# Sparse-attention and pooling block: one wide query projection, a padded value tile, probabilities scaled on GpSimd, weight-sum copies on the SyncE queue

## The chip, the core and the metric

The kernel runs on one core of one Trainium2 chip. The metric is device time in microseconds (us) of one execution; lower is better. TensorE (PE in the profile) multiplies matrices, VectorE (DVE), ScalarE (ACT) and GpSimd (POOL) work element by element, and DMAs are issued here by SyncE (SP) and by GpSimd, each in the order of its queue.

## What is computed

One decoder layer on x of 1024 positions by 1024 channels, all in float32. Attention has 8 query heads over 2 key/value heads and three branches; a pooling mixer runs beside it; both are gated, projected, added to x, and a squared-ReLU MLP of width 4096 follows.

```
h = rms_norm(x); proj = h @ w_in          # queries, 6 key/value sets, gates, pooling input, merge gates
a = g0*softmax(q k_cmp) v_cmp + g1*softmax(q k_sel) v_sel + g2*softmax(q k_win) v_win
a = a @ w_branch_attn
b = pool_mixer(u_pool) @ w_branch_pool    # trailing means over 2/4/8/16, group maps
x = x + (sigmoid(ga)*a + sigmoid(gb)*b) @ w_out
x = x + square(relu(rms_norm(x) @ w_ff1)) @ w_ff2
out = rms_norm(x)
```

With 16 blocks of 64 positions and 16 selected blocks, the selected branch is plain causal attention here, and the kernel computes it so.

## The kernel before

**Precision.** Each float32 operand is split in a high part (cast to fp32r by ACT) and a low part (the rest, by a subtraction), and `mm3` (lines 77 to 79) does three matmuls for one product: high by high, high by low, low by high. The helper `load` (L163 to L183) fetches a weight tile of 128x512 into a ring `wraw` of 4 buffers (L178), casts it to `whi` (L179) and subtracts to `wlo` (L82, on VectorE or, by default, on GpSimd); `whi` and `wlo` have 3 buffers each.

**Stages, in the order of time.** (1) Keys and values of four branches for all positions, and the row norms. (2) `block2` and `compress`: the other keys and values, and the two compressing MLPs. (3) `qblock(0)` and `qblock(1)`: the queries, 256 columns each; for every tile t of 128 positions 24 matmuls with a 256-column moving weight, then ACT scales the result into `q` (L394), GpSimd rotates it (`rope`, L145 to L149), and SP stores it in DRAM (`qd`). `keys` (rotation on VectorE, a transpose L362, a split) is called in the first pass only. (4) The pooling mixer and its gate `gb`, m = 0 to 7. (5) Attention: 32 pairs (i, hp), i being the block of 128 queries and hp the pair of heads. Query tiles come back from DRAM (`load_q`, L543) and are transposed and split by `split_q`. For each pair, `units_a` makes scores (L557, L558, masks L560), the row maxima (L567, VectorE), the exponentials (L568, ACT), and then scales the probabilities by gate over sum: selected ones in L624 and compressed ones in L625 on VectorE, window ones in L626 on ACT. `units_b` of the same pair then transposes the probabilities in blocks of 128 (L652), splits them (L655 ACT, L656 VectorE), and multiplies by the values (L663). The last block takes the compressed values `vch`, a tile of 64 rows (a "64x256" matmul on 64 of the array's rows). Pair n's `units_b` is interleaved with pair n+1's `units_a`. As filler, the merge gate `ga` is projected beside it: 128 terms of three 512-column matmuls each (`ga_terms`, tile `psG`), handed out by `advance` in proportion to the work done. (6) Branch projection, merge (`ta` and `gb` come back from DRAM, L803 and L804) and `w_out`, whose residual is loaded straight into `acc` (L817). (7) The MLP, in a scheme with 7 instead of 8 block products that needs sums of weight blocks.

**Weight sums.** `weight_sums` makes these sums by DMA alone, 32 tiles of 1 MB: a 16-byte token (L209, SP), which makes the step wait for a place in the program, then a DRAM to DRAM copy (L210, GpSimd queue), and one step later an accumulating DMA (L215, GpSimd queue). Seven steps run beside the pooling gate, 25 beside attention.

**What sets the order.** The program is written as above; the tile framework's scheduler then sets the order of each engine's instructions, and every engine runs its own list in that order. Pools give and take back on-chip memory; a tile waits until the one that lay there before has been read.

Of the kernel before, what the change touches and what calls it, by code (L numbers as in the profile page):

```python
# [49 lines left out]
def build(tc, a, out, dbg=None):  # L50
# [87 lines left out]

    def rope(eng, v, nh, cos, sin, wk):
        cb = cos[:, None, None, :].to_broadcast([P, nh, 2, 8])  # L140
        sb = sin[:, None, :].to_broadcast([P, nh, 8])
        A = wk.tile([P, 8, 2, 8], F32, name="ropeA", bufs=2)[:, :nh]
        B = wk.tile([P, 8, 2, 8], F32, name="ropeB", bufs=2)[:, :nh]
# [20 lines left out]
    def load(src, lo_eng=None, blk=None):  # L164
        _, na, n = src.shape
        step = min(na, HALF // n) if blk is None else 1
        his, los = [], []
        for a0 in range(0, na, step):
            w = step * n
            raw = strm.tile([P, HALF], F32, tag="wraw", name="wraw", bufs=RAWS)  # L170
            if blk is None:
                hi = strm.tile([P, HALF], F32R, tag="whi", name="whi", bufs=HILO)
                lo = strm.tile([P, HALF], F32R, tag="wlo", name="wlo", bufs=HILO)
            else:
                hi = blk.tile([P, 280], F32R, tag="bhi", name="bhi", bufs=10)
                lo = blk.tile([P, 280], F32R, tag="blo", name="blo", bufs=10)
# [10 lines left out]
    vst = [vk.tile([P, NT, NG, P], F32R, name=f"vst{b}") for b in range(2)]  # L187
    vch = vk.tile([DH, NG, P], F32R, name="vch")
    kds = vk.tile([P, NG, NCB + S], F32R, name="kds")
# [91 lines left out]
    with ExitStack() as st:  # L281
        psF = pool(st, "psF", bufs=4, space=PSUM)
        psH = pool(st, "psH", bufs=2, space=PSUM)
        wkA = pool(st, "wkA", side="right")

        def compress(kv):
            X = wkA.tile([P, 16, NG, NCB], F32, name="X")
            Xh = wkA.tile([P, 16, NG, NCB], F32R, name="Xh")
            Xl = wkA.tile([P, 16, NG, NCB], F32R, name="Xl")
            nc.gpsimd.memset(X[DH:P, :, :, NCB - 1:NCB], 0.0)  # L290
# [57 lines left out]
            else:  # L348
# [6 lines left out]
                for g in range(NG):  # L355
                    nc.vector.tensor_copy(vch[:, g], f(vh[g * DH:(g + 1) * DH]))

# [27 lines left out]

        def qblock(b):
            w = block_w(b * 256, 256)
            for t in range(NT):
                sl = slice(t * P, (t + 1) * P)
                ps = psF.tile([P, HALF], F32, name="psF")  # L390
                mm3(ps[:, :256], [(XH[k][:, sl], XL[k][:, sl], w[0][:, k], w[1][:, k])
                                  for k in range(NK)])
                q = wkA.tile([P, 4, 2, DH], F32, name="q", bufs=2)
                nc.scalar.activation(q, dup(ps[:, :256].rearrange("p (h d) -> p h d", d=DH)), AF.Copy,  # L394
                                     scale=req[:, t:t + 1])
                rope(nc.gpsimd, q.rearrange("p h e d -> p (h e) d"), 8, cosT[:, t], sinT[:, t], wkA)
                nc.sync.dma_start(qd[t][:, b * 512:(b + 1) * 512], q.rearrange("p h e d -> p (h e d)"))
# [13 lines left out]
        nc.vector.tensor_scalar(sg, sg, 0.5, 0.5, op0=MUL, op1=ADD)  # L411
        qblock(0)
        qblock(1)
        dump("kds", f(kds))
# [5 lines left out]
    kvctx.close()  # L420
    blkctx.close()


    with ExitStack() as st:
# [6 lines left out]
        with ExitStack() as st2:  # L431
# [79 lines left out]
    with ExitStack() as st:  # L511
# [13 lines left out]
        def ga_terms():  # L525
            for m in range(NK):
                gh, gl = load(cols(a["w_in"], C_GA + m * P, P))
                for hf in range(2):
# [10 lines left out]
                    yield  # L539

        def load_q(i, g):
            qi = wk.tile([P, HALF], F32, name="qi", bufs=2)
            nc.sync.dma_start(qi, qd[i][:, g * HALF:(g + 1) * HALF])  # L543
            return qi

# [47 lines left out]
        def unit_win(u, e):  # L593
# [19 lines left out]
            if e == 1:  # L613
# [22 lines left out]
        def units_b(u):  # L636
            i, hp, g, nw, w0 = (u[n] for n in ("i", "hp", "g", "nw", "w0"))
            blocks = [(u["pS"], NCB + b * P, vst[0][:, b, g], P) for b in range(i + 1)]
            blocks += [(u["pW"], b * P, vst[1][:, w0 + b, g], P) for b in range(nw // P)]
            blocks.append((u["pS"], 0, vch[:, g], NCB))  # L640
            o = oacc[:, hp % 2]
# [4 lines left out]
            def tr(gi):  # L646
                bl = groups[gi]
                n = len(bl)
                ps = psT.tile([P, HALF], F32, name="psT").rearrange("p (b e n) -> p b e n", b=2, e=2)
                for j, (src, c0, _, _) in enumerate(bl):  # L650
                    for e in range(2):
# [7 lines left out]
            def pv(gi):  # L659
                ph, pl = parts.pop(gi)  # L660
                for part in (ph, pl):
                    for j, (_, _, v, rows) in enumerate(groups[gi]):
                        nc.tensor.matmul(o, lhsT=v, rhs=part[:rows, j], start=gi == 0 and j == 0 and part is ph,  # L663
                                         stop=2 * gi + j == nb - 1 and part is pl)
# [22 lines left out]
        done, given, summed = 0.0, 0, 0  # L687

        def advance(w):
            nonlocal done, given  # L690
# [353 lines left out]
```

## Time and profile before

| what | us |
|---|---|
| median of 3 runs (lowest, highest) | 1493.94 (1491.46, 1497.39) |
| the profiled execution's own time | 1493.06 |
| its span | 1491.3 |
| PE, DVE, ACT, POOL busy | 1443.1, 1006.1, 759.2, 154.1 |

The span is the time from the first to the last recorded instruction. The profiled execution's own time is 1.8 us longer than its span, and stands 0.9 us below the median. Matmuls are pipelined: the recorded length of one is longer than the distance to the next, so distances between starts are read as its price.

### The profile page before, as it was taken

To read this page: it belongs to the slowest core of one execution; us is meant where nothing else is said; L and a number is where in the kernel's file an instruction comes from. 1 tells how busy PE (TensorE), PEld (TensorE's weight loads), DVE (VectorE), ACT (ScalarE), POOL (GpSimd) and SP (SyncE) were. 2 spreads that over 40 slices of the span, in tenths; PEclk is the share of its full clock that TensorE was granted. 3 is DMA by queue.
4 is the path that set the end of the run, shared out by engine and by line. 5 is a ranking of instruction groups with operands and counts; after the bars stand their busy time and mean duration, and the time that the engine had idled before them with its cause. 6 is when DMAs were issued, how large, how long until landed. Compare 5 with 4: busy or idle time off the path is not lost.

```text
span 1491.3 us, 20797 instructions
## 1 busy us (share of the span) xinstructions
PE 1443.1 (97%) x7385; PEld 1193.7 (80%) x7385; DVE 1006.1 (67%) x1950; ACT 759.2 (51%) x1559; POOL 154.1 (10%) x214
## 2 busy tenths in 40 slices
PE   8899999998999999999899999999999999999996
PEld 6788888886778887787688888888888888888885
DVE  5793461115888888787657658667897376669995
ACT  4454231124778877776334454575344454764451
POOL 2006423331111111111000000000000000000000
PEclk9999999999999999999999999999999999999998
DMA  8234217875768678766955332333233233333323
GB/s 309 69 100 149 71 43 189 215 202 132 201 156 212 153 187 196 171 169 150 327 174 162 108 97 91 100 100 99 85 106 97 94 99 93 99 94 97 98 80 113
DMA packets 130233, 204.67 MB, mean 137 GB/s; under 512 B 9936, under 2 KB 62928, under 8 KB 129616
## 3 DMA queue, kind: packets, MB, share of 16 engines
q1 hardware_dynamic: 112064, 136.22, 29.7%
q0 software_dynamic: 17920, 67.11, 19.9%
q8 instruction: 58, 0.95, 0.2%
q14 instruction: 47, 0.39, 0.1%
q10 hardware_dynamic: 144, 0.00, 0.0%
HBM read 186.52 MB, written 83.89 MB: 181 GB/s over the span
## 4 chain that ended last, share of the span: by engine, by line
PE 87%; DVE 5%; DMA 3%; ACT 2%; issue 1%; POOL 0%; SPq 0%; DVEq 0%; ACTq 0%; POOLq 0%
PE psm L79 16%; PE psm L77 16%; PE psm L78 16%; PE oacc L663 6%; PE psF L78 5%; PE psF L79 5%; PE psF L77 5%; PE psT L652 4%; PE psS L557 3%; PE psS L558 2%; PE psG L77 2%; PE psG L78 2%; PE psG L79 2%; DMA gb<-gbd 1%; PE psS L560 1%
## 5 line engine op out<-in xcount | busy, mean ns | idle before, releaser
L77 PE MATMUL psm<-mv,whi 128*128 128x512 f32 x896 | 350.6, 391 | 0.0
L78 PE MATMUL psm<-mv,whi 128*128 128x512 f32 x896 | 350.6, 391 | 0.0
L79 PE MATMUL psm<-mv,wlo 128*128 128x512 f32 x896 | 350.5, 391 | 0.0
L866 ACT CAST whi<-wraw 128x512 fp32r<-128x512 f32 x224 | 138.9, 621 | 257.6 <-PE psm L78 193.0
L82 DVE TENSOR_TENSOR wlo<-wraw,whi 128x512 fp32r<-128x512 f32 x288 | 196.7, 686 | 90.7 <-ACT whi L866 70.0
L78 PEld LDWEIGHTS psm<-mv,whi 128*128 128x128 f32 x896 | 168.3, 188 | 36.8
L77 PEld LDWEIGHTS psm<-mv,whi 128*128 128x128 f32 x896 | 168.3, 188 | 36.7
L79 PEld LDWEIGHTS psm<-mv,wlo 128*128 128x128 f32 x896 | 168.3, 188 | 36.7
L179 ACT CAST whi<-wraw 128x512 fp32r<-128x512 f32 x112 | 69.7, 622 | 122.2 <-PE psF L78 57.9
L656 DVE TENSOR_TENSOR pl<-psT,ph 128x512 fp32r<-128x512 f32 (+1 forms) x160 | 101.9, 646 | 30.3 <-ACT ph L655 29.0
L655 ACT CAST ph<-psT 128x512 fp32r<-128x512 f32 (+1 forms) x160 | 87.7, 556 | 49.4 <-PE psT L652 47.6
L567 DVE TENSOR_REDUCE nm<-psS 128x1 f32<-128x64 f32 (+8 forms) x192 | 99.8, 539 | 17.4 <-PE psS L560 10.2
L82 POOL TENSOR_TENSOR wlo<-wraw,whi 128x512 fp32r<-128x512 f32 x48 | 65.5, 1367 | 120.3 <-ACT whi L179 100.0
L77 PE MATMUL psF<-xh,whi 128*128 128x512 f32 x192 | 74.7, 389 | 0.0
L78 PE MATMUL psF<-xl,whi 128*128 128x512 f32 x192 | 74.7, 389 | 0.0
L79 PE MATMUL psF<-xh,wlo 128*128 128x512 f32 x192 | 74.7, 389 | 0.0
L568 ACT ACTIVATE pS<-psS,nm 128x64 f32<-128x64 f32 (+8 forms) x128 | 67.9, 532 | 8.8 <-DVE nm L567 8.3
L846 ACT CAST mv<-mt 128x512 fp32r<-128x512 f32 x96 | 59.1, 617 | 15.9 <-DVE mt L844 11.4
L82 DVE TENSOR_TENSOR mv<-mt,mv 128x512 fp32r<-128x512 f32 x96 | 65.0, 684 | 1.1 <-ACT mv L846 0.6
L663 PE MATMUL oacc<-ph,vst 128*128 128x256 f32 x264 | 64.0, 317 | 1.2 <-ACT ph L655 0.9
L652 PE MATMUL psT<-cf,pS 128*128 128x128 f32 x352 | 60.5, 276 | 2.7 <-DVE pS L624 2.6
L77 PE MATMUL psF<-bhi,xh 128*128 128x256 f32 (+1 forms) x192 | 55.6, 293 | 5.7 <-DVE vst L270 4.4
(248 smaller groups left out, 2970.0 us busy)
## 6 DMA issues: line engine op xcount, KB each, us to landing
wraw<-wsw_ff SPq DMA_DIRECT2D x128, 256.0 KB
wraw<-in_w_ff SPq DMA_DIRECT2D x96, 256.0 KB
wsw_ff<-in_w_ff POOLq DMA_DIRECT2D x16, 1024.0 KB, 9.1
wsw_ff<-wsw_ff POOLq DMA_DIRECT2D x16, 1024.0 KB, 9.5
wraw<-in_w_in SPq DMA_DIRECT2D x40, 256.0 KB
wraw<-in_w_out SPq DMA_DIRECT2D x32, 256.0 KB
xt<-in_x SPq DMA_DIRECT2D x8, 512.0 KB
qd<-q SPq DMA_DIRECT2D x16, 256.0 KB
```

The costliest lines, as they stand in the source:

```text
L77: nc.tensor.matmul(ps, lhsT=sh, rhs=mh, start=first and i == 0, stop=False, skip_group_check=more)
L78: nc.tensor.matmul(ps, lhsT=sh, rhs=ml, start=False, stop=False, skip_group_check=more)
L79: nc.tensor.matmul(ps, lhsT=sl, rhs=mh, start=False, stop=last and i == n - 1, skip_group_check=more)
L82: eng.tensor_tensor(lo, src, f(hi), op=SUB)
L179: nc.scalar.copy(h, v)
L567: nc.vector.tensor_reduce(nm, v, axis=AX.X if flat else AX.XY, op=MAX, negate=True)
L568: nc.scalar.activation(p if flat else p.rearrange("p (a n) -> p a n", a=2), v, AF.Exp, bias=nm, accum_out=sm)
L652: nc.tensor.transpose(ps[:, j, e], src[e][:, c0:c0 + P], ident)
L655: nc.scalar.copy(ph[:, :n], ps[:, :n])
L656: nc.vector.tensor_tensor(pl[:, :n], ps[:, :n], f(ph[:, :n]), op=SUB)
L663: nc.tensor.matmul(o, lhsT=v, rhs=part[:rows, j], start=gi == 0 and j == 0 and part is ph, stop=2 * gi + j == nb - 1 and part is pl)
L866: nc.scalar.copy(hi, raw)
```

## The change

- `qblock` runs once with 512 columns: 8 tiles of 24 matmuls; `keys` is called for each of its tiles. Its weights lie in a pool `qb` of 7 buffers that takes the place of `compress`'s large tiles, and one tile more in the ring.
- The first two query tiles are loaded back before the pooling gate starts, from a pool `qp` of their own.
- `vch` has 128 rows, the lower 64 being zero, and its matmul uses all 128.
- Selected probabilities are scaled on GpSimd.
- The weight-sum copies go to the SP queue. Three steps run beside the pooling mixer's input, eight beside its gate, and 21 beside attention, whose steps are handed out over the first 85% of the work.
- 20 filler terms are handed out at the start of attention, and 16 kept for its end.
- In `w_out` the residual is loaded into a buffer of the ring `wraw` and not into `acc`.

```diff
-    vch = vk.tile([DH, NG, P], F32R, name="vch")
+    vch = vk.tile([P, NG, P], F32R, name="vch")
+    nc.gpsimd.memset(f(vch[DH:P]), 0.0)
@@ weight_sums
                         nc.sync.dma_start(d[0:1, 0:4], made.pop())
-                        nc.gpsimd.dma_start(d, a[layer][fh, m0, k0, h])
+                        nc.sync.dma_start(d, a[layer][fh, m0, k0, h])
@@ qblock
-        def qblock(b):
-            w = block_w(b * 256, 256)
+        def qblock():
+            w7 = load(cols(a["w_in"], C_Q, HALF, 0, 7), nc.vector, qb)
+            w1 = load(cols(a["w_in"], C_Q, HALF, 7, 1), nc.vector)
+            w = [Parts(w7[e].tiles + w1[e].tiles) for e in range(2)]
             for t in range(NT):
...
-                mm3(ps[:, :256], [(XH[k][:, sl], XL[k][:, sl], w[0][:, k], w[1][:, k])
-                                  for k in range(NK)])
+                mm3(ps, [(XH[k][:, sl], XL[k][:, sl], w[0][:, k], w[1][:, k]) for k in range(NK)])
+                for b in range(2):
...
-                if b == 0:
-                    keys(t, 0, kds[:, :, NCB + t * P:NCB + (t + 1) * P])
-                elif t in (2, 5):
+                keys(t, 0, kds[:, :, NCB + t * P:NCB + (t + 1) * P])
+                if t in (2, 5):
@@ pooling mixer
             for m in (3, 2, 1, 0):
                 cur = pool_in(m)
+                if made:
+                    next(sums)
+                made[:] = [f(cur[1])[0:1, 0:4]]
...
+            qi = [load_q(0, 0), load_q(0, 1)]
@@ unit_win
-                    nc.vector.tensor_scalar(pS[:, NCB:NCB + ns], pS[:, NCB:NCB + ns], c[:, e_, 1:2], None, op0=MUL)
+                    nc.gpsimd.tensor_scalar(pS[:, NCB:NCB + ns], pS[:, NCB:NCB + ns], c[:, e_, 1:2], None, op0=MUL)
@@ units_b
-                        nc.tensor.matmul(o, lhsT=v, rhs=part[:rows, j], start=gi == 0 and j == 0 and part is ph,
+                        nc.tensor.matmul(o, lhsT=v, rhs=part[:, j], start=gi == 0 and j == 0 and part is ph,
@@ advance
-        LAG = 1
+        LAG, FIRST, LAST = 1, 20, 16
...
-            while given < nterm and given < nterm * done / total:
+            if len(bseq) and n >= len(pairs) - 1:
+                ending += 0.4 * LAST / nslot
+            while given < nterm and given < FIRST + (nterm - FIRST - LAST) * done / total + ending:
...
-            if n >= 2 and summed < 25 * done / total:
+            if n >= 2 and len(wsum) < 32 and summed < 22 * done / total / 0.85:
@@ w_out
-                nc.sync.dma_start(acc[:, m, sl], a["xT"][m * P:(m + 1) * P, sl])
+                xt = strm.tile([P, HALF], F32, tag="wraw", name="wraw", bufs=RAWS)
+                nc.sync.dma_start(xt, a["xT"][m * P:(m + 1) * P, sl])
...
-                nc.vector.scalar_tensor_tensor(acc[:, m, sl], ps, 0.5, acc[:, m, sl], op0=MUL, op1=ADD)
+                nc.vector.scalar_tensor_tensor(acc[:, m, sl], ps, 0.5, xt, op0=MUL, op1=ADD)
```

How the change moves instructions, at three places. In the changed kernel the lines from 190 on are one to fifteen higher: L557, L558, L560 become L569, L570, L572; L652 and L663 become L664 and L675; L624 becomes L636, L210 and L215 become L211 and L216.

POOL, attention, before, blocks i = 5 and 6 (`wsw_ff` are the sum tiles, "16x16384" a copy, "512x512" an accumulation):

```order
L82 TENSOR_TENSOR wlo<-wraw,whi 128x512
L215 DMA wsw_ff_6362<-in_w_ff 512x512
L210 DMA wsw_ff_6536<-in_w_ff 16x16384
L215 DMA wsw_ff_6536<-wsw_ff_5844 512x512
L210 DMA wsw_ff_6713<-in_w_ff 16x16384
L215 DMA wsw_ff_6713<-wsw_ff_6029 512x512
L210 DMA wsw_ff_6887<-in_w_ff 16x16384
L82 TENSOR_TENSOR wlo<-wraw,whi 128x512
```

POOL in the changed kernel, the same blocks:

```order
L636 TENSOR_SCALAR pS<-pS,cc 128x768 x2
L82 TENSOR_TENSOR wlo<-wraw,whi 128x512
L216 DMA wsw_ff_6140<-wsw_ff_5819 512x512
L636 TENSOR_SCALAR pS<-pS,cc 128x768 x2
L216 DMA wsw_ff_6294<-wsw_ff_5970 512x512
L636 TENSOR_SCALAR pS<-pS,cc 128x896 x2
L216 DMA wsw_ff_6485<-in_w_ff 512x512
L636 TENSOR_SCALAR pS<-pS,cc 128x896 x2
L82 TENSOR_TENSOR wlo<-wraw,whi 128x512
L216 DMA wsw_ff_6648<-in_w_ff 512x512
```

The copies are gone from this queue, and every pair's two scalings now stand between accumulations and splits of filler weights.

PE at the start of attention, before (`psF` is the pooling gate, `psG` a filler term, `qi` a query tile to be transposed, `psS` scores):

```order
L79 MATMUL psF<-mxh,wlo 128x512
L77 MATMUL psG<-xh_65,whi 128x512
L78 MATMUL psG<-xl_73,whi 128x512
L79 MATMUL psG<-xh_65,wlo 128x512
L77 MATMUL psG<-xh_66,whi 128x512
L78 MATMUL psG<-xl_74,whi 128x512
L79 MATMUL psG<-xh_66,wlo 128x512
L77 MATMUL psG<-xh_67,whi 128x512
L78 MATMUL psG<-xl_75,whi 128x512
L549 MATMUL psT<-cf,qi 128x128 x4
```

PE in the changed kernel, from the same last `psF` matmul:

```order
L79 MATMUL psF<-mxh,wlo 128x512
L77 MATMUL psG<-xh_65,whi 128x512
L569 MATMUL psS<-kds,qh 128x192
L569 MATMUL psS<-kdw,qh 128x128
L569 MATMUL psS<-kds,qh 128x192
L570 MATMUL psS<-kds,ql 128x192
```

The transposes of the first query tile have moved far ahead, into the pooling stage; the scores come first, and 23 filler matmuls stand between them and the first transposes of probabilities.

PE at the start of the last pair's transposes, before:

```order
L663 MATMUL oacc<-ph,vst_98 128x256
L663 MATMUL oacc<-ph,vch 128x256
L77 MATMUL psG<-xh_67,whi 128x512
L663 MATMUL oacc<-pl,vst_98 128x256
L663 MATMUL oacc<-pl,vch 128x256
L78 MATMUL psG<-xl_75,whi 128x512
L79 MATMUL psG<-xh_67,wlo 128x512
L652 MATMUL psT<-cf,pS 128x128 x2
L77 MATMUL psG<-xh_68,whi 128x512
L78 MATMUL psG<-xl_76,whi 128x512
```

PE in the changed kernel, there:

```order
L675 MATMUL oacc<-ph,vst_98 128x256
L675 MATMUL oacc<-ph,vch 128x256
L675 MATMUL oacc<-pl,vst_98 128x256
L675 MATMUL oacc<-pl,vch 128x256
L664 MATMUL psT<-cf,pS 128x128 x8
L675 MATMUL oacc<-ph,vst_97 128x256 x2
```

No filler stands there any more: all 128 terms have been issued before.

## Rows read from the trace of the kernel before

**Rows 1.** Stages: window, us, busy us of PE, PEld, DVE, ACT, POOL, clock, DMA, GB/s.
```profile
104.20:158.20 54.00, 50.35 (x410) 48.59 (x410) 21.13 (x93) 23.08 (x55) 28.29 (x78) 1.00 0.43 132
339.20:353.80 14.60, 8.71 (x46) 6.70 (x45) 4.15 (x18) 4.34 (x19) 1.28 (x1) 0.88 0.69 174
353.80:694.90 341.10, 334.93 (x2174) 272.07 (x2175) 277.07 (x649) 260.55 (x659) 53.25 (x59) 1.00 0.73 175
...
706.20:745.20 39.00, 31.57 (x118) 24.15 (x118) 24.53 (x42) 14.65 (x27) 1.53 (x2) 0.91 1.07 320
745.20:852.90 107.70, 107.67 (x483) 88.83 (x484) 70.02 (x117) 43.77 (x72) 0.00 (x0) 1.00 0.49 150
```

**Rows 2.** Timeline of PE (start, us), in the query stage and in the pooling stage.
```profile
110.32 0.28 PE L79 MATMUL psF<-bhi,xl 128*128 128x256 f32 x1
110.44 0.28 PE L77 MATMUL psF<-bhi,xh 128*128 128x256 f32 x1
...
200.20 0.39 PE L79 MATMUL psF<-xh,wlo 128*128 128x512 f32 x1
200.43 0.39 PE L77 MATMUL psF<-xh,whi 128*128 128x512 f32 x1
```

**Rows 3.** Waits of PE, 104 to 159 us: total us, times, longest.
```profile
PE psT L362 <- DVE kvA L149: 2.2, 4, 1.0
PE psF L77 <- ACT bhi L179: 1.4, 1, 1.4
```

**Rows 4.** Timeline of PE at the start of attention; in brackets the idle time before.
```profile
346.65 0.90 PE L549 MATMUL psT<-cf,qi 128*128 128x128 f32 x4 [4.02 <-DMA qi<-qd]
...
353.77 0.90 PE L652 MATMUL psT<-cf,pS 128*128 128x128 f32 x3 [0.67 <-DVE pS L624]
```

**Rows 5.** Timeline of PE at the end of one pair, with `vch`.
```profile
676.58 0.27 PE L663 MATMUL oacc<-ph,vst 128*128 128x256 f32 x1
676.78 0.38 PE L663 MATMUL oacc<-ph,vch 64*128 64x256 f32 x1
677.09 0.38 PE L663 MATMUL oacc<-pl,vst 128*128 128x256 f32 x1
677.41 0.38 PE L663 MATMUL oacc<-pl,vch 64*128 64x256 f32 x1
677.72 0.50 PE L557 MATMUL psS<-kds,qh 128*128 128x512 f32 x1
```

**Rows 6.** One line's instructions, ns min/median/max; then groups: busy us, mean ns | idle.
```profile
L624 DVE TENSOR_SCALAR pS<-pS,cc x64: 277/514/754, 353.4 to 694.3; 128x128 f32<-128x128 f32 x8, 128x256 f32<-128x256 f32 x8, 128x384 f32<-128x384 f32 x8, 128x512 f32<-128x512 f32 x8
...
L82 POOL TENSOR_TENSOR wlo<-wraw,whi 128x512 fp32r<-128x512 f32 x48 | 65.5, 1367 | 120.3 <-ACT whi L179 100.0 <-PE psG L79 11.3 <-ACT pS L568 4.6
L145 POOL TENSOR_TENSOR ropeA<-q,cf 128x128 f32<-128x128 f32 x16 | 7.4, 462 | 38.9 <-ACT q L394 38.9
```

**Rows 7.** Timeline of VectorE and POOL at one pair's scalings (start, us).
```profile
425.56 0.41 DVE L624 TENSOR_SCALAR pS<-pS,cc 128x384 f32<-128x384 f32 x1
425.66 1.46 POOL L82 TENSOR_TENSOR wlo<-wraw,whi 128x512 fp32r<-128x512 f32 x1 [11.34 <-PE psG L79]
425.89 1.29 DVE L625 TENSOR_SCALAR pS<-pS,cc 128x64 f32<-128x64 f32 x1
...
427.43 0.24 DVE L625 TENSOR_SCALAR pS<-pS,cc 128x64 f32<-128x64 f32 x1
```

**Rows 8.** Waits of POOL, whole span.
```profile
POOL wsw_ff L215 <- DMA wsw_ff<-in_w_ff: 80.4, 18, 9.4
```

**Rows 9.** Waits of VectorE, 706 to 746 us.
```profile
DVE ta L805 <- DMA ta<-tad: 7.1, 2, 4.3
```

**Rows 10.** A load of 128x280 in the chain of waits (us); cast and subtraction of 128x512.
```profile
43.33 2.72 DMA wraw<-in_w_in
...
L179 ACT CAST whi<-wraw 128x512 fp32r<-128x512 f32 x112 | 69.7, 622 | 122.2 <-PE psF L78 57.9 <-PE psm L78 42.1 <-issue 7.6
L82 DVE TENSOR_TENSOR mv<-mt,mv 128x512 fp32r<-128x512 f32 x96 | 65.0, 684 | 1.1 <-ACT mv L846 0.6
```

More of the change, by code (lines that the diff above doesn't have):

```diff
@@ L137, in bcast, with rope @@
         nc.scalar.copy(dst, ps[:, :n * P])
-    def rope(eng, v, nh, cos, sin, wk):
+    def rope(eng, v, nh, cos, sin, wk, tag=""):
         cb = cos[:, None, None, :].to_broadcast([P, nh, 2, 8])
         sb = sin[:, None, :].to_broadcast([P, nh, 8])
-        A = wk.tile([P, 8, 2, 8], F32, name="ropeA", bufs=2)[:, :nh]
-        B = wk.tile([P, 8, 2, 8], F32, name="ropeB", bufs=2)[:, :nh]
+        A = wk.tile([P, 8, 2, 8], F32, name="ropeA" + tag, bufs=2)[:, :nh]
+        B = wk.tile([P, 8, 2, 8], F32, name="ropeB" + tag, bufs=2)[:, :nh]
         x = v[:, :, 0:16].rearrange("p h (b e) -> p h b e", b=2)
@@ L174, in load @@
             else:
-                hi = blk.tile([P, 280], F32R, tag="bhi", name="bhi", bufs=10)
-                lo = blk.tile([P, 280], F32R, tag="blo", name="blo", bufs=10)
+                hi = blk.tile([P, n], F32R, tag="bhi", name="bhi", bufs=8 if n < HALF else 7)
+                lo = blk.tile([P, n], F32R, tag="blo", name="blo", bufs=8 if n < HALF else 7)
             v, h, l = raw[:, :w], hi[:, :w], lo[:, :w]
@@ L284, in build @@
         wkA = pool(st, "wkA", side="right")
+        xctx = ExitStack()
+        xp = pool(xctx, "xp", side="right")
         def compress(kv):
-            X = wkA.tile([P, 16, NG, NCB], F32, name="X")
-            Xh = wkA.tile([P, 16, NG, NCB], F32R, name="Xh")
-            Xl = wkA.tile([P, 16, NG, NCB], F32R, name="Xl")
+            X = xp.tile([P, 16, NG, NCB], F32, name="X")
+            Xh = xp.tile([P, 16, NG, NCB], F32R, name="Xh")
+            Xl = xp.tile([P, 16, NG, NCB], F32R, name="Xl")
             nc.gpsimd.memset(X[DH:P, :, :, NCB - 1:NCB], 0.0)
@@ L355, in compress @@
                 for g in range(NG):
-                    nc.vector.tensor_copy(vch[:, g], f(vh[g * DH:(g + 1) * DH]))
+                    nc.vector.tensor_copy(vch[0:DH, g], f(vh[g * DH:(g + 1) * DH]))
         def keys(t, br, dst):
@@ L390, in qblock @@
                 ps = psF.tile([P, HALF], F32, name="psF")
-                mm3(ps[:, :256], [(XH[k][:, sl], XL[k][:, sl], w[0][:, k], w[1][:, k])
-                                  for k in range(NK)])
[L393 to L397, printed above, removed]
-                if b == 0:
-                    keys(t, 0, kds[:, :, NCB + t * P:NCB + (t + 1) * P])
-                elif t in (2, 5):
+                mm3(ps, [(XH[k][:, sl], XL[k][:, sl], w[0][:, k], w[1][:, k]) for k in range(NK)])
+                for b in range(2):
+                    q = wkA.tile([P, 4, 2, DH], F32, name="q", bufs=2)
+                    nc.scalar.activation(q, dup(ps[:, b * 256:(b + 1) * 256].rearrange("p (h d) -> p h d", d=DH)),
+                                         AF.Copy, scale=req[:, t:t + 1])
+                    rope(nc.gpsimd, q.rearrange("p h e d -> p (h e) d"), 8, cosT[:, t], sinT[:, t], wkA, "q")
+                    nc.sync.dma_start(qd[t][:, b * 512:(b + 1) * 512], q.rearrange("p h e d -> p (h e d)"))
+                keys(t, 0, kds[:, :, NCB + t * P:NCB + (t + 1) * P])
+                if t in (2, 5):
                     hf = t // 3
@@ L411, in build @@
         nc.vector.tensor_scalar(sg, sg, 0.5, 0.5, op0=MUL, op1=ADD)
-        qblock(0)
-        qblock(1)
+        xctx.close()
+        qb = pool(st, "qb", side="right")
+        qblock()
         dump("kds", f(kds))
@@ L421, in build, with load_q @@
     blkctx.close()
+    qctx = ExitStack()
+    qp = pool(qctx, "qp")
+    def load_q(i, g):
+        qi = qp.tile([P, HALF], F32, name="qi", bufs=2)
+        nc.sync.dma_start(qi, qd[i][:, g * HALF:(g + 1) * HALF])
+        return qi
     with ExitStack() as st:
@@ L539, in ga_terms @@
                     yield
[L541 to L544, printed above, removed]
         def split_q(qi):
@@ L637, in units_b @@
             i, hp, g, nw, w0 = (u[n] for n in ("i", "hp", "g", "nw", "w0"))
-            blocks = [(u["pS"], NCB + b * P, vst[0][:, b, g], P) for b in range(i + 1)]
-            blocks += [(u["pW"], b * P, vst[1][:, w0 + b, g], P) for b in range(nw // P)]
-            blocks.append((u["pS"], 0, vch[:, g], NCB))
+            blocks = [(u["pS"], NCB + b * P, vst[0][:, b, g]) for b in range(i + 1)]
+            blocks += [(u["pW"], b * P, vst[1][:, w0 + b, g]) for b in range(nw // P)]
+            blocks.append((u["pS"], 0, vch[:, g]))
             o = oacc[:, hp % 2]
@@ L649, in tr @@
                 ps = psT.tile([P, HALF], F32, name="psT").rearrange("p (b e n) -> p b e n", b=2, e=2)
-                for j, (src, c0, _, _) in enumerate(bl):
+                for j, (src, c0, _) in enumerate(bl):
                     for e in range(2):
@@ L661, in pv @@
                 for part in (ph, pl):
-                    for j, (_, _, v, rows) in enumerate(groups[gi]):
-                        nc.tensor.matmul(o, lhsT=v, rhs=part[:rows, j], start=gi == 0 and j == 0 and part is ph,
+                    for j, (_, _, v) in enumerate(groups[gi]):
+                        nc.tensor.matmul(o, lhsT=v, rhs=part[:, j], start=gi == 0 and j == 0 and part is ph,
                                          stop=2 * gi + j == nb - 1 and part is pl)
@@ L686, in build @@
         total, nterm = sum(weight), 2 * NK * NK
-        done, given, summed = 0.0, 0, 0
+        done, given, summed, ending = 0.0, 0, 0, 0.0
         def advance(w):
-            nonlocal done, given
+            nonlocal done, given, ending
             done += w
-            while given < nterm and given < nterm * done / total:
+            if len(bseq) and n >= len(pairs) - 1:
+                ending += 0.4 * LAST / nslot
+            while given < nterm and given < FIRST + (nterm - FIRST - LAST) * done / total + ending:
                 next(fill, None)
                 given += 1
-        qi = load_q(0, 0)
-        q = split_q(qi)
-        qnext = load_q(0, 1)
+        q = split_q(qi[0])
+        qnext = qi[1]
         bseq, bw = [], 0
@@ L743, in build @@
     psTctx.close()
+    qctx.close()
     attn.close()
```

## The prediction

> **What bounds the kernel now.** I read the stage table first [rows 1], then PE's timeline for the true pitch of a matmul [rows 2], then the waits and timelines where PE stands idle [rows 3 to 5, 9], and last the durations of what moves between engines [rows 6, 7]. The first thing to see is that PE is the bound: 1443.1 us busy in a span of 1491.3, 107.67 of 107.70 in `w_out` and 334.93 of 341.10 in attention [rows 1]. So a gain must be fewer or shorter matmul slots, or the end of a place where PE idles. Two such places stand out: the start of attention (8.71 busy of 14.60) and the passage from attention to `w_out` (31.57 of 39.00). Both also have a granted clock below 1.00 (0.88 and 0.91), after the idle time.
>
> The second thing to see is the pitch. Recorded lengths overlap, so I take start to start: 0.12 us for 256 columns, 0.23 for 512 [rows 2]. Two 256-column matmuls cost 0.01 more than one of 512.
>
> **The change, part by part.** The sum is made against the profiled execution's own 1493.06 us (its span plus 1.8); this is 0.9 below the median, so the median should land as much above the sum.
>
> *One query pass: -4.4.* Before, 384 matmuls of 0.12 give 46.1 of the stage's 54.0 us [rows 1, 2]; now 192 of 0.23 give 44.2: -1.9. The second pass's wait for its first cast weights, 1.4, goes with the pass [rows 3]: -1.4. PE's transposes waited 2.2 in four places for the rotated keys [rows 3]; `keys` now has 24 x 0.23 = 5.5 us per tile instead of 24 x 0.12 = 2.9, so half of that at least goes: -1.1. The two rotations of queries per tile take the same time on GpSimd as before, now spread over one pass.
>
> *Query tiles ahead: -7.* PE stood 4.02 us for the first query tile to come back from DRAM and 0.67 for the first scaled probabilities [rows 4]; in all it is idle 14.60 - 8.71 = 5.9 us in this stage, and its clock of 0.88 costs 0.12 x 14.60 = 1.75 [rows 1]. At most 7.6 can go. Now the transposes lie in the pooling stage, and 23 filler matmuls (23 x 0.23 = 5.3 us) cover the first softmax. I take -7; the lower bound is the tile's wait alone, -4.
>
> *Padded `vch`: -13.* Each pair has 4 matmuls with `vch`, in two places or one. In the timeline starts go 676.58, .78, 677.09, .41, .72: 0.20, then 0.31 three times, where 256 columns else take 0.12 [rows 5]. The excess is 0.08 + 3 x 0.19 = 0.65 where 64-row and 128-row matmuls alternate. Over 32 pairs that is at most 21 us; where the `vch` matmuls stand together there is one entry and one exit (0.08 + 0.19), over 32 pairs 8.6. They alternate in 14 pairs and stand together in 18: 14 x 0.65 + 18 x 0.27 = 14, of which I take 13, since not every place shows all of it. The bounds are -21 and 0, the latter if the excess is not from the rows and stays.
>
> *Scaling on GpSimd: +13.* VectorE loses 64 scalings of 0.277 to 0.754 us, median 0.514, some 33 us [rows 6]. GpSimd has no such one-operand instruction before. Its nearest rows are two-operand ones: 462 ns at 128 elements, 1367 at 512 [rows 6], so 2.36 ns per element over a base of 0.16. At the mean of 576 elements this would be 1.52 us; if each operand read costs half of the slope, 0.16 + 1.18 x 576/1000 = 0.84. There is more to it. Where a GpSimd split of 1.46 us ran beside the scalings, VectorE's 64-element scaling took 1.29 instead of 0.24 us and ended with it [rows 7]: VectorE was held up while GpSimd worked. The Trainium skill states this as a rule ("SBUF — State Buffer", SBUF: two separate sides): the two engines share a port pair, and the one that starts first keeps it for its whole instruction. It speaks against this change: a scaling moved off VectorE can still hold VectorE up, and by it the 33 us are not freed at all. The trace agrees in these rows.
>
> So a pair's path from its factors to its transposes was 2 x (0.514 + 0.24) = 1.5 us, and becomes 2 x (0.84 + 0.24) = 2.2, the compressed scalings (L637) standing between those on GpSimd: +0.7 a pair, and at the last three blocks (768 to 1024 elements, 1.07 to 1.37 us against 0.61 to 0.75) about +1.1. In blocks 0 to 4 the new order puts some 23 us more of PE work, over 20 pairs, between the last scores and the first transposes: 1.15 each, which covers 0.7. In blocks 5 to 7 it puts none there, and before, PE started its transposes as the scaling ended. So 12 pairs x 1.1 = +13. I count no relief of VectorE, since it is held instead. The ends: two-operand price, nothing covered, 2 x (1.52 + 0.24) - 1.5 = 2.0 x 32 = +64; GpSimd as quick as VectorE and VectorE freed of half a scaling per exposed pair, -6.
>
> *Weight sums: +1.* Copies no longer stand in GpSimd's queue, which waited 80.4 us in 18 places for them before the accumulations [rows 8]. The accumulations remain there, each now one step behind its copy, so that it should find it landed; one that doesn't holds the scalings behind it. On SP, a copy waits for its token, and the weight, query and `ta` loads stand behind it; a load takes 2.72 us [rows 10] and is asked for a ring of buffers ahead. 0 to +6 by two such loads; I take +1.
>
> *Filler: +2.* The last pair loses its 15 filler matmuls (15 x 0.23 = 3.45), and the start has them instead, where they are counted above. What they covered at the end is the wait for scalings: 0 to +3.5, taken +2.
>
> *Passage to `w_out`: -9.* PE is idle 39.00 - 31.57 = 7.4 there, and the clock of 0.91 costs 0.09 x 39.00 = 3.5: at most -10.9 [rows 1]. DMA is busy all through (share 1.07, 320 GB/s) [rows 1], with the last copies and accumulations among it, and `ta` is awaited for 7.1 us on VectorE [rows 9]. Handing the sums out by 85% of the work ends them some 50 us earlier. I take -9; the lower bound is -5, if the loads of the merge remain late by themselves.
>
> *`w_out`'s residual in the ring: +3.* Now a residual holds one of 4 buffers until the end of its step, and the weights of the step after next wait for that: addition 0.68, load 2.72, cast 0.62, split 0.68 [rows 10], 4.7 us against a step of 24 x 0.23 = 5.5. A slack of 0.8 hides it; a load that is late by a few tenths uses it up. 0 to +14 (14 steps of 1 us), taken +3.
>
> **The sum**: -4.4 - 7 - 13 + 13 + 1 + 2 - 9 + 3 = -14.4, so 1478.7; as a median, 0.9 higher, 1480.
>
> **The rivals.** (A) GpSimd scales at VectorE's price, or what stands before the transposes covers it: the +13 goes, 1467. For it: five blocks have the cover already. Against: all GpSimd rows are over twice as slow per element. The Trainium skill has such a rule ("GPSIMD Engine Reference", 4.1 Engine selection): about half VectorE's speed with two inputs, near line rate with one. No run here shows a one-input instruction on GpSimd.
>
> (B) The other side: the scaling costs the two-operand price, and VectorE, held through every one of them, hands the splits (L668) and maxima to PE late in all blocks. All exposed, it is 1467 + 64 = 1531. It decides when more than +34 is exposed (1467 + 34 = 1501), that is 1.1 us per pair or a mean scaling of 1.05 us. For it: the held-up row [rows 7], and VectorE 277.07 of 341.10 us busy [rows 1]. Against: the fillers that now lie ahead of the transposes.
>
> (C) The padding buys nothing, since the excess comes from changing the weights and not from the rows: 1480 + 13 = 1493. Against: only places with 64-row weights show 0.20 and 0.31 [rows 5]. The Trainium skill says that the row count doesn't matter for a weight load ("TensorE: Matmul & The Clock Gate", Step-by-step: what each phase is for); the starts here differ with it.
>
> (D) `w_out` starves in its ring: +14 instead of +3, 1491. For it: slack of 0.8 only. Against: all loads of the stage have a free queue by then (DMA share 0.49 [rows 1]).
>
> **How the numbers follow.** Forecast 0.42, own range 1472 to 1487; A 0.20; B 0.14; C 0.04; D 0.12; the rest, 0.08, is mixtures near 1487, half on either side. A measurement here can tell about 0.5% from no change, 7.5 us: faster is below 1486.5, slower above 1501.4. Faster: 0.42 + 0.20 + 0.04 = 0.66. Same: 0.12 + 0.04 + 0.04 = 0.20. Slower: B, 0.14. The range goes down to 1454, which is A with the padding at its upper bound and the other terms near theirs, and up to 1504, which takes in C and D and the beginning of B; most of B and a little below are left out.
>
> **What would show it.** The query stage at a pitch of 0.23 without the 1.4 wait. No wait for `qi` and a clock of 1.00 at the start of attention. Starts of `vch` matmuls 0.12 apart. The scalings (L636): a mean near 0.84 us confirms the term, 0.5 makes it A, 1.5 B; with it the length of L637 (0.24 free, near L636's when held) and PE's waits for `pS` before the transposes (L664), which should lie in blocks 5 to 7. Waits of GpSimd for copies at L216 above 1 us would move the blame to the queue. From attention's end to `w_out`, a DMA share well below 1.07 and no long wait for `ta`. In `w_out`, PE waits on cast weights mean D. I am wrong in the main if attention, from its first scores to its last matmul, is longer by more than 10 us in spite of `vch`.

## The result, and the profile after

The changed kernel took 1545.87 us (median of 4 runs, 1536.68 to 1552.40) beside 1493.16 before: a ratio of 1.0344, 95% interval 1.0285 to 1.0403. It is slower by 53 us, where 1480 was forecast, and lies above the stated range of 1454 to 1504. The profiled execution has a span of 1545.7 us.

First the stage table of the changed kernel (columns as in [rows 1]). Its first window is not quite the query stage: the first query matmul starts at 104.36 us and the first one of the pooling input at 153.85.

```profile
103.20:155.20 52.00, 51.78 (x239) 40.59 (x238) 22.19 (x90) 21.18 (x50) 25.94 (x75) 1.00 0.42 132
...
336.30:343.60 7.30, 7.17 (x39) 6.02 (x40) 3.36 (x13) 2.96 (x15) 3.63 (x4) 1.00 0.95 150
343.60:757.00 413.40, 354.70 (x2192) 288.23 (x2191) 263.76 (x593) 266.04 (x665) 145.09 (x96) 0.93 0.57 139
757.00:771.50 14.50, 10.34 (x57) 8.67 (x57) 5.47 (x10) 5.18 (x10) 2.70 (x1) 0.76 0.14 40
...
812.00:918.00 106.00, 106.00 (x485) 87.68 (x485) 67.75 (x115) 44.59 (x75) 0.00 (x0) 1.00 0.53 163
```

All of the loss lies in one stage. The stretches below are bounded by PE's first filler matmul, the first matmul of the branch projection (L77, `psm`) and the first one of the following row norm (L782, before L768); times and differences in us:

| stretch | before | after | predicted | measured |
|---|---|---|---|---|
| to the first filler matmul | 340.5 | 336.3 | -4.4 | -4.2 |
| attention | 367.1 | 435.2 | -4 | +68.1 |
| branch projection to row norm | 98.6 | 89.5 | -6 | -9.1 |

The -4 of attention is the sum of start -7, `vch` -13, scaling +13, copies +1 and filler +2; -6 is -9 + 3. Before and after this stage the steps came out; in attention PE is busy 354.70 of 413.40 us, and its granted clock is 0.93 instead of 1.00. The prediction named its own sign of being wrong in the main, attention longer by more than 10 us, and it has come.

The groups of GpSimd in the changed kernel, by shape, answer to [rows 6] (busy us, mean ns of one, then idle time before).

```profile
L636 POOL TENSOR_SCALAR pS<-pS,cc 128x1024 f32<-128x1024 f32 x8 | 22.8, 2860 | 49.9 <-DVE cc L631 49.9
...
L636 POOL TENSOR_SCALAR pS<-pS,cc 128x512 f32<-128x512 f32 x8 | 12.6, 1575 | 7.5 <-DVE cc L631 7.5
...
L636 POOL TENSOR_SCALAR pS<-pS,cc 128x128 f32<-128x128 f32 x8 | 4.7, 600 | 17.3 <-DVE cc L631 7.4 <-ACT pW L580 5.7 <-ACT qh L564 4.1
```

All 64 together are busy 110.7 us, 1.76 in the mean: not 0.84, and more than the two-operand price of 1.52 that stood as the upper end. From 128 to 1024 elements it is (2860 - 600) / 896 = 2.52 ns per element over a base of 0.28 us. VectorE took 0.28 to 0.75 us for the same tiles.

Then the waits of the changed kernel ([rows 8] before): GpSimd's for copies, PE's longest, and PE's for the splits that VectorE makes (L668).

```profile
POOL wsw_ff L216 <- DMA wsw_ff<-in_w_ff: 114.7, 22, 13.3
...
PE psT L664 <- POOL pS L636: 56.6, 44, 3.7
...
PE oacc L675 <- DVE pl L668: 1.1, 5, 0.2
```

Before, PE's transposes waited for scaled probabilities 2.6 us in all:

```profile
PE psT L652 <- DVE pS L624: 2.6, 4, 1.1
```

One pair shows how the wait comes about; this is the chain of waits from 694.5 us on.

```profile
694.54 0.18 DVE cc L631
...
694.90 5.71 POOL pS L636 x2
...
700.66 0.47 PE psT L664
```

The factors are ready at 694.72, GpSimd scales for 5.71 us without a pause, and then the transposes start. Over the whole chain L636 has 5.1% of 1545.7, some 79 us. But GpSimd also stands 114.7 us in its queue for copies, and the prediction had said that such waits at L216 would move the blame to the queue. So it had to be settled which of the two it was: the price of the instruction, or what it stands behind.

The changed kernel's trace already speaks to it. In 29 of the 32 pairs GpSimd starts the first scaling 0.17 to 0.20 us after the end of the factors (L631); in the other three it starts 0.5, 2.5 and 4.9 us after. So what stood ahead in the queue held the scalings for some 7 us in all, most of it behind one accumulation whose copy had not landed.

### The profile page after: what moved, and what is told of

The parts are those of the page before. It is cut to its first block, busy times and chain, and to the rows that moved or that the text cites. A ratio compares the mean times of both kernels' runs of the same rounds, so it can differ in the third digit from the quotient of the medians.

```text
span 1545.7 us, 20563 instructions
## 1 busy us (share of the span) xinstructions
PE 1456.9 (94%) x7193; PEld 1198.3 (78%) x7193; DVE 991.3 (64%) x1878; ACT 760.5 (49%) x1551; POOL 248.5 (16%) x247
## 4 chain that ended last, share of the span: by engine, by line
PE 63%; POOL 5%; DVE 2%; ACT 2%; DMA 1%; issue 1%; POOLq 0%; DVEq 0%; ACTq 0%; SPq 0%
PE psm L79 16%; PE psm L78 16%; PE psm L77 16%; POOL pS L636 5%; PE psT L664 4%; PE oacc L675 4%; PE psS L569 2%; PE psS L570 1%; DMA wsw_ff<-in_w_ff 1%; PE psG L77 1%; PE psG L79 1%; PE psG L78 1%; DVE nm L579 1%; ACT pS L580 1%; PE psS L572 1%
## 5 line engine op out<-in xcount | busy, mean ns | idle before, releaser
L77 PE MATMUL psm<-mv,whi 128*128 128x512 f32 x896 | 350.6, 391 | 0.0
L77 PEld LDWEIGHTS psm<-mv,whi 128*128 128x128 f32 x896 | 168.3, 188 | 36.6
L668 DVE TENSOR_TENSOR pl<-psT,ph 128x512 fp32r<-128x512 f32 (+1 forms) x160 | 102.0, 648 | 70.4 <-ACT ph L667 69.0
L636 POOL TENSOR_SCALAR pS<-pS,cc 128x128 f32<-128x128 f32 (+7 forms) x64 | 110.7, 1755 | 150.6 <-DVE cc L631 94.2
L664 PE MATMUL psT<-cf,pS 128*128 128x128 f32 x352 | 72.2, 316 | 56.7 <-POOL pS L636 56.6
L664 PEld LDWEIGHTS psT<-cf,pS 128*128 128x128 f32 x352 | 47.3, 161 | 71.8 <-POOL pS L636 71.2
L77 PE MATMUL psF<-xh,whi 128*128 128x512 f32 x192 | 74.8, 390 | 0.0
L675 PE MATMUL oacc<-ph,vst 128*128 128x256 f32 x264 | 67.6, 337 | 0.2
```

Source lines behind the costliest of these rows:

```text
L77: nc.tensor.matmul(ps, lhsT=sh, rhs=mh, start=first and i == 0, stop=False, skip_group_check=more)
L636: nc.gpsimd.tensor_scalar(pS[:, NCB:NCB + ns], pS[:, NCB:NCB + ns], c[:, e_, 1:2], None, op0=MUL)
L664: nc.tensor.transpose(ps[:, j, e], src[e][:, c0:c0 + P], ident)
L668: nc.vector.tensor_tensor(pl[:, :n], ps[:, :n], f(ph[:, :n]), op=SUB)
L675: nc.tensor.matmul(o, lhsT=v, rhs=part[:, j], start=gi == 0 and j == 0 and part is ph, stop=2 * gi + j == nb - 1 and part is pl)
```

## The experiments

Theory: GpSimd's own time per scaling is the loss (price). Rivals: the scalings are held up behind accumulations (queue), or the rest of the change costs it.

**1. Scaling back on VectorE.**

```diff
-                    nc.gpsimd.tensor_scalar(pS[:, NCB:NCB + ns], pS[:, NCB:NCB + ns], c[:, e_, 1:2], None, op0=MUL)
+                    nc.vector.tensor_scalar(pS[:, NCB:NCB + ns], pS[:, NCB:NCB + ns], c[:, e_, 1:2], None, op0=MUL)
```

> The changed kernel with the selected scaling back on VectorE, all else as changed. Theory (price): GpSimd's own 1.755 us per scaling, two in a row for each pair, is the loss. The idle time of TensorE that the trace puts to these scalings, 56.6 us, and the 0.07 of clock over 413.4 us of attention, 29 us, go: about 1460, and in any case 1455 to 1475, 19 to 38 us faster than before; the granted clock in attention is 1.00. Rival (queue): the scalings wait behind accumulations whose copies have not landed; the time would fall as far, so this run alone does not tell the two apart. Rival (the rest of the change costs it: fillers moved, copies on SP): stays above 1493.

Measured 1473.18 us, ratio to before 0.9857 (0.9834 to 0.9880): faster than before, and 73 us faster than the change with this one line. So the rest of the change does not cost the loss. The time lies in the range of 1455 to 1475, though 13 us above "about 1460". Attention takes 361.3 us, in two stretches of its trace:

```profile
337.60:533.40 195.80, 189.01 (x1246) 154.69 (x1247) 157.53 (x417) 149.54 (x425) 30.09 (x26) 1.00 0.76 186
533.40:698.90 165.50, 158.38 (x1040) 130.32 (x1038) 133.34 (x265) 122.57 (x267) 13.47 (x11) 0.97 0.57 136
```

and the same two, blocks 0 to 4 and 5 to 7, in the changed kernel:

```profile
336.30:558.90 222.60, 196.99 (x1250) 160.22 (x1250) 145.39 (x378) 151.71 (x426) 80.75 (x67) 0.97 0.68 165
558.90:771.50 212.60, 175.22 (x1036) 142.70 (x1036) 127.20 (x239) 122.47 (x265) 70.68 (x34) 0.87 0.44 104
```

PE's idle time is 13.9 us in the one and 63.0 in the other, +49; the rest of the 74 us, +25, is busy time for the same number of matmuls, at a granted clock of 0.97 and 0.87 where the first run has 1.00 and 0.97. And +27 of the 74 falls in blocks 0 to 4, where the prediction counted on cover.

**2. The kernel before, with the scaling on GpSimd** (the same edit the other way, in L624).

> The kernel before with the selected scaling on GpSimd and nothing else. Price theory: attention grows by about as much as the changed kernel's did beyond the rest of the change, 1545.9 - 1460 = some 86 us, to about 1579. Queue rival: here copies too stand in GpSimd's queue, where they waited 149.9 us for tokens and the accumulations 80.4 us for copies; scalings behind them would wait that too, and the time would be above 1620. Rival (the rest of the change costs it): below 1510.

Measured 1576.57 us, 1.0543 (1.0517 to 1.0569), +81: the price theory's 1579, and far from the queue's 1620. In its waits PE loses about as much to scalings as in the changed kernel, though copies (L210, which wait for their tokens) and accumulations (L215) both stand in GpSimd's queue; there too, in 28 of 32 pairs, the first scaling starts 0.17 to 0.20 us after the factors:

```profile
POOL wsw_ff L215 <- DMA wsw_ff<-in_w_ff: 55.5, 15, 6.5
...
PE psT L652 <- POOL pS L624: 50.5, 50, 2.5
...
POOL wsw_ff L210 <- DMA wsw_ff<-oT: 34.0, 8, 9.2
```

**3. One head on GpSimd, the other on VectorE.**

```diff
-                    nc.gpsimd.tensor_scalar(pS[:, NCB:NCB + ns], pS[:, NCB:NCB + ns], c[:, e_, 1:2], None, op0=MUL)
+                    (nc.gpsimd, nc.vector)[e_].tensor_scalar(pS[:, NCB:NCB + ns], pS[:, NCB:NCB + ns], c[:, e_, 1:2], None, op0=MUL)
```

> The changed kernel with the scaling of a pair's second head back on VectorE, so that the two run side by side. Price theory: a pair's path is one GpSimd scaling instead of two, 1.755 instead of 3.5 us; half of the 86 us goes, more if the fillers cover a first one: 1485 to 1505. Queue rival: the first head's scaling still stands behind the accumulations, and at most 10 us go: 1535 or more.

Measured 1503.56 us, 1.0057 (1.0041 to 1.0072), within the price theory's range: half the scalings, somewhat over half of the loss gone.

**4. Accumulations a step later.**

```diff
-                        if len(late) > 1:
+                        if len(late) > 2:
```

> The changed kernel with each accumulation issued two steps behind its copy instead of one, so that GpSimd's queue finds the copy landed. Price theory: the two pieces of copies in the chain of waits, 12.6 and 9.8 us, are all that goes: 1520 to 1545. Queue rival: GpSimd's waits for copies, 114.7 us in 22, held the scalings, and most of the 86 us goes: below 1490.

Measured 1543.73 us, 1.0328 (1.0297 to 1.0358), at the upper end of the price theory's 1520 to 1545. The edit did less than meant: GpSimd still waits at its accumulations, and the same few scalings start late (2.7 and 5.2 us after their factors).

```profile
POOL wsw_ff L216 <- DMA wsw_ff<-in_w_ff: 97.8, 18, 13.5
...
PE psT L664 <- POOL pS L636: 56.5, 45, 4.0
```

By itself this run is weak evidence. With the second run and the starts of the scalings it speaks against the queue: GpSimd's waits for copies changed by 17 us and PE's for scalings not at all.

**5. `vch` on 64 rows again**, with the scaling on VectorE (its tile, the row count in `blocks` and in the matmul as before).

> The first run's kernel (scaling on VectorE, all else as changed; 1473.2 us) with the compressed values back on 64 rows. If the rows cost: the starts around the matmuls with these values lie 0.12 us apart by the trace of the first run and did not in the kernel before; summed over all of them the excess was 12.2 us there and is 3.0 here, so +9, 1482; by the prediction's term +13, 1486. If the padding buys nothing: 1473 within 2 us.

Measured 1483.87 us, 0.9912 (0.9890 to 0.9935), 10.7 more than the first run and between the two figures expected; attention itself is 368.6 instead of 361.3. The padding is worth some 7 to 11 us. In the first run's timeline of PE the starts around `vch` are as 256 columns have them elsewhere, 0.11 to 0.12 ([rows 5] before):

```profile
481.29 0.40 PE L675 MATMUL oacc<-pl,vst 128*128 128x256 f32 x2
481.53 0.28 PE L675 MATMUL oacc<-ph,vch 128*128 128x256 f32 x1
481.64 0.28 PE L675 MATMUL oacc<-pl,vch 128*128 128x256 f32 x1
481.76 0.40 PE L77 MATMUL psG<-xh,whi 128*128 128x512 f32 x1
```

**6. Less filler at the start**, scaling on VectorE.

```diff
-        LAG, FIRST, LAST = 1, 20, 16
+        LAG, FIRST, LAST = 1, 8, 0
```

> The first run's kernel with 8 instead of 20 filler terms handed out at the start and none kept for the end. In the first run's order the last three stretches of attention have 7, 0 and 0 filler matmuls and lose 17 us beyond their matmul slots, in the kernel before (24, 12, 15) 8 us; here they are 19, 11, 14, and the first stretch keeps its 24. Theory (the end lacks filler): 9 us go, 1464. Rival (the fillers at the start are worth as much): 1473 or more.

Measured 1472.94 us, 0.9841 (0.9817 to 0.9866): the theory's 1464 did not come, the rival's figure did. Attention is 361.3 us as in the first run. First this run's start and end of attention, then the first run's:

```profile
336.60:380.00 43.40, 37.86 (x226) 31.87 (x226) 30.21 (x107) 28.68 (x108) 7.80 (x7) 0.88 0.73 171
...
655.00:697.90 42.90, 40.72 (x274) 34.12 (x272) 34.28 (x69) 30.12 (x62) 0.00 (x0) 1.00 0.06 19
```

```profile
337.60:381.00 43.40, 40.73 (x245) 32.97 (x245) 27.83 (x99) 27.50 (x104) 8.44 (x7) 1.00 0.65 165
...
655.00:698.90 43.90, 38.34 (x232) 31.01 (x231) 32.08 (x62) 28.07 (x59) 0.00 (x0) 0.88 0.09 26
```

The hole moved from the end to the start, and the low clock with it (0.88 at either place). The 384 filler matmuls are a fixed stock.

**7. The scaling in another form on GpSimd**, a product with the factor repeated along the row.

```diff
-                    nc.gpsimd.tensor_scalar(pS[:, NCB:NCB + ns], pS[:, NCB:NCB + ns], c[:, e_, 1:2], None, op0=MUL)
+                    nc.gpsimd.tensor_tensor(pS[:, NCB:NCB + ns], pS[:, NCB:NCB + ns], c[:, e_, 1:2].to_broadcast([P, ns]), op=MUL)
```

> The changed kernel with each GpSimd scaling written as a two-operand multiplication by the factor repeated along the row, instead of a multiplication by one factor per partition. If the two-operand rows hold for it (462 ns at 128 elements, 1288 at 512): 2.2 ns per element over 0.19, 1.45 us in the mean against 1.755, and 0.4 times the 0.3 less per scaling and pair that shows at full length, 64 x 0.3 = 20, at most: 1526 to 1540. If the price is that of any GpSimd pass with a factor: 1540 to 1552.

Measured 1525.36 us, 1.0181 (1.0154 to 1.0209), 20 us less than the changed kernel and just below the range of 1526 to 1540. The form is quicker than expected (GpSimd's groups by shape):

```profile
L636 POOL TENSOR_TENSOR pS<-pS,cc 128x1024 f32<-128x1024 f32 x8 | 15.1, 1909 | 44.3 <-DVE cc L631 44.3
...
L636 POOL TENSOR_TENSOR pS<-pS,cc 128x128 f32<-128x128 f32 x8 | 3.0, 398 | 15.0 <-DVE cc L631 9.1 <-ACT pW L580 5.9
```

That is 1.69 ns per element instead of 2.52. But the time saved on GpSimd is partly lost on VectorE. PE's waits for scalings fall from 56.6 to 21.5 us, and its waits for VectorE's work grow (for these splits, from 1.1 to 5.8):

```profile
PE psT L664 <- POOL pS L636: 21.5, 30, 1.9
...
PE oacc L675 <- DVE pl L668: 5.8, 10, 2.8
```

Timeline of this run, then of the changed kernel, at a pair of the last block:

```profile
699.09 3.83 DVE L637 TENSOR_SCALAR pS<-pS,cc 128x64 f32<-128x64 f32 x2
699.13 3.74 POOL L636 TENSOR_TENSOR pS<-pS,cc 128x1024 f32<-128x1024 f32 x2 [10.32 <-DVE cc L631]
```

```profile
712.79 1.28 DVE L637 TENSOR_SCALAR pS<-pS,cc 128x64 f32<-128x64 f32 x2
712.85 5.72 POOL L636 TENSOR_SCALAR pS<-pS,cc 128x1024 f32<-128x1024 f32 x2 [12.24 <-DVE cc L631]
...
715.80 0.33 PE L664 MATMUL psT<-cf,pS 128*128 128x128 f32 x1 [1.91 <-POOL pS L636]
...
718.62 0.90 PE L664 MATMUL psT<-cf,pS 128*128 128x128 f32 x3 [1.57 <-POOL pS L636]
```

In the first, VectorE's two scalings of 64 elements end with GpSimd's pair, 3.83 us for 0.5; over the run L637 takes 1058 ns in the mean. In the second they take 1.28 beside 5.72: they are held for a part of it.

**8. Weight sums over the whole of attention**, scaling on VectorE.

```diff
-            if n >= 2 and len(wsum) < 32 and summed < 22 * done / total / 0.85:
+            if n >= 2 and len(wsum) < 32 and summed < 22 * done / total:
```

> The first run's kernel with the weight sums of attention handed out over the whole of it instead of its first 85%. Theory (the gain of 9 us in the passage to the output projection comes from copies and accumulations ending earlier): the stretch from the first matmul of the branch projection to the row norms' one goes from 89.6 back towards 98.6, the time to 1477 to 1482. Rival (it comes from the residual's new buffer or the queue): 1473 within 2.

Measured 1472.35 us, 0.9831 (0.9804 to 0.9857): no loss, but this shows nothing on the passage, since the edit missed its aim: SP issued the last copy at 670.6 and GpSimd the last accumulation at 677.2, both before attention's end at 697.0.

**9. The last sums after attention's end** (the factor 22 / 0.85 of that line becomes 18).

> The first run's kernel with the weight sums of attention handed out more slowly (18 instead of 22 / 0.85 per unit of work), so that the last two copies and three accumulations wait for attention's end, as in the kernel before. (In the run with late sums SP had still issued its last copy 26 us before attention's end, so it put none there.) Theory (those 1 MB transfers stood beside the merge's loads and cost the passage its 9 us): from the first matmul of the branch projection to the row norms' one 89.6 becomes 95 to 99, 1478 to 1483 in all. Rival: 89.6 within 1, 1473 within 2.

Measured 1486.72 us, 0.9930 (0.9908 to 0.9952), 13.5 more than the first run and above the theory's 1478 to 1483. The last copies are issued at 699 and 700, the last accumulations at 708 and 711. The passage (from the first matmul of the branch projection to the row norm's) and VectorE's wait in it ([rows 9] before):

```profile
695.80:798.40 102.60, 94.86 (x386) 74.67 (x386) 61.79 (x98) 36.32 (x62) 2.05 (x2) 0.95 0.78 227
```

```profile
DVE ta L819 <- DMA ta<-tad: 10.9, 4, 4.1
```

The passage is 102.6 us, where 89.6 was the first run's, 98.6 the kernel's before, and 95 to 99 expected. So the tail of the sums does lengthen it, here by more than the 9 us that it was to explain: the cause is shown, its size is overshot.

**10. The residual loaded straight into its accumulator**, scaling on VectorE (L831 to L835 as before).

> The first run's kernel with the residual loaded straight into its accumulator again. Its loads of 256 KB are then asked for as early as the place is free, twelve of them before the kernel before had passed from attention to the projection, ahead of loads that the merge needed. Theory (these loads cost the passage its 9 us): 89.6 becomes 95 to 99, 1478 to 1483. Rival (the sums' tail did it): 89.6 within 1, and 1473 or, with a ring buffer more for the weights, 1470.

Measured 1476.47 us, 0.9865 (0.9841 to 0.9888); the passage is 90.4 us, not 95. The rival holds: the residual's place does not matter there. The time is 3 us above the rival's 1473, with an interval that overlaps the first run's.

**11. One head on GpSimd in the quicker form.**

```diff
-                    nc.gpsimd.tensor_scalar(pS[:, NCB:NCB + ns], pS[:, NCB:NCB + ns], c[:, e_, 1:2], None, op0=MUL)
+                    if e_ == 0:
+                        nc.gpsimd.tensor_tensor(pS[:, NCB:NCB + ns], pS[:, NCB:NCB + ns],
+                                                c[:, e_, 1:2].to_broadcast([P, ns]), op=MUL)
+                    else:
+                        nc.vector.tensor_scalar(pS[:, NCB:NCB + ns], pS[:, NCB:NCB + ns], c[:, e_, 1:2], None, op0=MUL)
```

> The first run's kernel with the first head's scaling on GpSimd as a two-operand multiplication (1.15 us in the mean in the run where both were) and the second head's on VectorE. If VectorE is held for as long as GpSimd works (in that run its 64-element scalings took 1.06 instead of 0.29 us), VectorE's scalings come behind: 1.15 + 0.51 + 2 x 0.29 = 2.2 us a pair instead of 1.6, 0.6 x 32 = 20 us at most: 1478 to 1493. If the two engines work side by side: 1.15 + 0.29 = 1.4 us, and VectorE is relieved: 1462 to 1473.

Measured 1500.19 us, 1.0032 (1.0012 to 1.0051): above both ranges. The timeline at one pair of the last block:

```profile
661.28 1.95 POOL L637 TENSOR_TENSOR pS<-pS,cc 128x1024 f32<-128x1024 f32 x1 [5.37 <-DVE cc L631]
661.38 2.39 DVE L640 TENSOR_SCALAR pS<-pS,cc 128x1024 f32<-128x1024 f32 x1
663.27 0.14 PEld L668 LDWEIGHTS psT<-cf,pS 128*128 128x128 f32 x1 [1.41 <-POOL pS L637]
```

VectorE's scaling, 0.75 us alone, took 2.39 and ends 0.54 after GpSimd's: for the most part the two ran one behind the other. The estimate of 20 us compared the ends of both scalings; but PE's first transpose needs only the first head's, which VectorE used to have ready after 0.75 and GpSimd has after 1.95. That first wait (1.41 us in the last row) may explain the rest; it is not shown, since the heads were not exchanged.

The first, sixth and eighth run (1473.2, 1472.9, 1472.4) beat both kernels; their intervals overlap.

## Why the prediction was wrong

**The step that failed** is *Scaling on GpSimd: +13*. By the first run beside the change it is 1545.9 - 1473.2 = +73, and the same line put into the kernel before costs +81. Three parts of the term were mis-sized. The price: "if each operand read costs half of the slope", 0.84 us, is 1.76; the mean stands outside the bounds that the rows of two-operand instructions gave, since the one-operand form is the dearer one (2.52 ns per element against 2.36 in [rows 6]). The cover: "1.15 each, which covers 0.7" fell with it, 27 us being lost in blocks 0 to 4; two scalings of 0.6 to 1.9 us are not covered by 1.15. And the clock was left out: PE's idle time is +49, the slower clock +25. Standing behind accumulations, which the prediction had under *Weight sums*, is some 7 us of this waiting at most.

**VectorE held up** [rows 7] was right in kind, but too large: "it is held instead" was to cost all of the relief. With the one-operand form L637 grew from 290 to 425 ns in the mean, 9 us in all, and VectorE is busy 272.6 us in attention instead of 290.9 in the first run, so more than half of the 33 us were freed. That bought nothing, since PE had hardly waited for VectorE. The holding is no constant either: with the product form L637 took 1058 ns. The rule of the Trainium skill ("SBUF — State Buffer", SBUF: two separate sides), held for the whole instruction, agrees with the product form (3.83 beside 3.74 us) and not with the one-operand form (1.28 beside 5.72). In the changed kernel PE waited 56.6 us for GpSimd's scalings and 1.1 for VectorE's splits.

**Rival B** had one half right: a price at the upper end of the bounds, exposed in all blocks, with a mean of 1.05 us per scaling as the point of decision; at 1.76 it was far past that. Its other half, splits that VectorE hands over late, did not come (1.1 us). With 1.76 its formula gives 2 x (1.76 + 0.24) - 1.5 = 2.5, times 32 = 80, and 1467 + 80 = 1547. That this is near the measured 1545.87 is luck: the formula has no clock and covers nothing, and the trace has +49 of waiting and +25 of clock. The 0.14 that B was given beside 0.42 for the forecast rested on the halved slope, for which no row spoke. **Rival A** is refuted: the scalings took 600 to 2860 ns on GpSimd, where VectorE had taken 277 to 754. The rule beside it ("GPSIMD Engine Reference", 4.1 Engine selection, of the Trainium skill), near line rate with one input, differs from the measured 2860 ns at 1024 elements, against 754 at most on VectorE [rows 6]; the measurement decides.

**The other steps.** Without the scaling the sum said 1467; the first run gives 1473. In attention the sum without it is -17, and the first run's 361.3 us beside 367.1 is -5.8. *One query pass* (-4.4): from the first query matmul to the first one of the pooling input it is 49.5 us instead of 54.2, -4.7, in the changed kernel and in the first run, with both waits of [rows 3] gone. *Query tiles ahead* (-7) and *filler* (+2) are one step, not two: from the first filler to the second pair it went from 19.1 us to 21.7 with 46 filler matmuls more, 46 x 0.23 = 10.6, so 8 were gained; but the last three stretches of the first run, with 7 filler matmuls instead of 51, lost 17 us beyond their matmul slots where they had lost 8 (an estimate, from starts in the two traces). Together that is about nothing. The sixth run shows it for the filler, whose place changes nothing; the query tiles were not tried alone. *Padded `vch`* (-13): 7 to 11 by the fifth run; rival C is refuted. A pair has two matmuls with `vch`, not four; the sum went by the starts and is not touched by this. *Passage* (-9): -9.1, and the reason given is borne out by the ninth run, though not its size. *Residual in the ring* (+3): nothing to be seen; PE is busy 106.00 of 106.00 us in that stage, and rival D is refuted. *Copies on SP* (+1) were not tried alone.

## What to carry to other kernels

Price a moved operation by its own form on its new engine; where no row shows that form, the nearest one is no upper bound, and the step must keep its whole range. A step on the path just ahead of the bounding engine cost twice here: the wait (+49), and the slower clock that came with it (+25). When a queue shows long waits, look at when the work behind them became ready: here the scalings of 29 of 32 pairs began at once, in spite of 114.7 us of waits. Filler is a fixed stock: putting it in one hole opens another.

## What was not expected of the hardware

- GpSimd multiplies 128x1024 by one factor per partition in 2860 ns, by the factor repeated as a second operand in 1909; at 128 elements in 600 and 398.
- How long GpSimd holds VectorE depends on GpSimd's form: two 64-element scalings took 1.28 us beside the first form (5.72) and 3.83 beside the second (3.74).
- PE's granted clock fell from 1.00 to 0.50 (from 2.4 to 1.2 GHz) in 12 stretches of the changed kernel's attention, 68 us in all, and in two of the kernel before, 7 us. It cost half as much again as the idle time (+25 beside +49).
